# A two-block network on one core: two attentions get lanes of their own, memory rows another queue, and gathers are counted by their indices

## The chip, the core and the metric

The program runs on one core of a Trainium2 chip. Its engines are TensorE (PE; its weight loads are PEld), VectorE (DVE), ScalarE (ACT), GpSimd (POOL) and SyncE (SP), each with a queue of its own that is worked off in order; transfers are started from SP's, ACT's or POOL's queue and run on 16 DMA engines. The metric is the time of one execution in microseconds of device time.

## What is computed

The input is 256 tokens of width 1024. A first network runs two layers (retention, then differential attention), each followed by a product-key expert layer; a second network then runs gated linear attention (GLA) and latent attention (MLA) side by side, cross attention to a memory of 256 rows, and a feed-forward block. The expert layer picks 8 x 16 = 128 rows of two tables per token:

```python
idx = jnp.take_along_axis(cidx, pos, axis=-1).reshape(PEER_CHUNK, PEER_HEADS * PEER_TOPK)
gate = jax.nn.softmax(top, axis=-1).reshape(PEER_CHUNK, PEER_HEADS * PEER_TOPK)
u_e = jnp.take(u, idx, axis=0)
v_e = jnp.take(v, idx, axis=0)
act = jax.nn.gelu(jnp.einsum('ted,td->te', u_e, xc).astype(jnp.float32))
return jnp.einsum('te,ted->td', (gate * act).astype(v_e.dtype), v_e)
...
o_mla = from_heads(causal_block_attention(q, k, v))
h = h + jnp.concatenate([o_gla, o_mla], axis=-1) @ w_out[l]
hn = rms_norm(h, norm_xa[l])
mn = rms_norm(mem, norm_mem[l])
```

## The kernel before, in words

Tokens are worked in two tiles of 128. The expert layers make four phases of 128 slots each: layer 0 of tile 0 and of tile 1, then layer 1 of tile 0 and of tile 1. A slot gathers one row of u and v side by side for each of 128 tokens (tile `g`, 128 x 2048 floats, 1.05 MB) by an indirect DMA from POOL (line 1103). There are eight `g` buffers; in the last phase one of them holds `xr`, so seven serve gathers. A slot then passes three stations. DVE multiplies the u half with the token and sums it (`g,pd<-g,xr`, line 1122; called a dot below). For each pair of slots ACT makes the gelu's terms (`pd<-pd`, lines 1125 and 1128), DVE the weight (`pw`, line 1137), and ACT two diagonal matrices from it (`dg`, line 1143). PE adds the v halves to the output with them (`Y<-g,dg`, line 275), and after that the buffer is free and POOL may issue the next gather.

Everything else runs beside these phases: routing, both attentions of layer 1, and in the last phase the memory's keys and values (`mem_kv`), the entry to the second network for tile 0 (`c_open`), and tile 0's GLA and MLA. Each of these is a Python generator in a lane. While the program is built, `experts` chooses after each step what comes next from a model of the engines (`Clock`): a ready dot, a ready `pw` with its products (`sums`), or a step of a side lane whose own data are ready by the model. What it chooses is the fixed order of each engine's queue. After a step the lane's wait time is set by what the generator yielded: a weight's job, a constant (LC), or nothing, which means the end of everything the step wrote.

In `mem_kv` one step both starts the load of 128 memory rows (`mx`, from SP, line 1332) and puts their squaring (`rms,ss<-mx`, line 625) into ACT's queue; a later step puts the reciprocal root on DVE (`rsqrt`, lines 352 to 366) and the scaling by it on ACT (line 628). `c_gla` and `c_mla` of tile 0 are one lane, zipped: each step of the lane takes a step of both, and inside `c_gla` the gates' products are zipped with `gla`. `rot` in `mla` (a product and six rope instructions on DVE, lines 1767 and 1386 to 1391) is part of a single step.

After the last phase tile 1 goes through `c_open`, GLA, MLA and, zipped with them, the rest of tile 0; cross attention and feed-forward follow. PE also gets filler products into an accumulating bank (`Y<-cst,zero`, line 271) where the model sees it idle.

Of the kernel before, what the change touches and what calls it, by code (L numbers as in the profile page):

```python
# [18 lines left out]
T = 256  # L19
# [151 lines left out]
LC, HP = 1, 2  # L171
# [5 lines left out]
QUEUE = 2.0  # L177
# [104 lines left out]
class Net:  # L282
# [560 lines left out]
    def route_open(self, t, l):  # L843
        if t == l == 0:
            xT = yield from self.xT_of(self.X[t], gain=self.col("ln_g0"), off=self.col("ln_b0"))
        elif t == l:
            xT = yield from self.xT_of(self.X[t])
        elif l == 0:
            xT = self.tl("om", D, name="rxT").rearrange("p (b t) -> p b t", b=8)
            yield from self.transp(self.X[t], xT, 8)  # L850
        else:
            xT = self.tl("om", D, name="rxT").rearrange("p (b t) -> p b t", b=8)
            yield from self.transp(self.X[t], xT, 8)
        idx = self.tl("idx", 128, I32, bufs=2)
        gate = self.tl("gate", 128, bufs=2)
        self.routed[t, l] = [idx, gate, 0, xT]
        yield

    def pq0_first(self):
# [72 lines left out]
    def route_t(self, t, l, s2, heads=(0, 1)):  # L932


        nc, V = self.nc, self.nc.vector
        idx, gate, n0, _ = self.routed[t, l]
        nh = len(heads)
        nb, ns = 2 * nh, 16 * nh
        sc = s2[:, :nb * 128].rearrange("p (b n) -> p b n", b=nb)
# [45 lines left out]
        to = lambda a, s, j: a[64 * s:64 * s + 64, n0:n0 + ns].rearrange("p (q j) -> p q j", j=2)[:, :, j]  # L985
        for s, j, _, r, c in spots:
            V.scalar_tensor_tensor(to(idx, s, j), part[0][r, c], float(NK), part[1][r, c], op0=OP.mult, op1=OP.add)
        ga = self.small(ns, name="ga").rearrange("p (h k) -> p h k", h=nh)
        V.tensor_tensor(ga, top, top[:, :, 0:1].to_broadcast([128, nh, 16]), op=OP.subtract)
        nc.scalar.activation(ga, ga, AF.Exp)  # L990
# [5 lines left out]
        gf = ga.rearrange("p h k -> p (h k)")  # L996
        for s, j, _, r, c in spots:
            V.tensor_scalar(to(gate, s, j), gf[r, c], gs[r, s * nh // 2:s * nh // 2 + 1], None, op0=OP.mult)
        self.routed[t, l][2] = n0 + ns
        yield  # L1000

    def route(self, t, l, i, heads=(0, 1)):
# [43 lines left out]
    def experts(self, phases, first, beside):  # L1046
# [4 lines left out]
        nc, V, clk = self.nc, self.nc.vector, self.clk  # L1051
        seq = [(p, n) for p in range(len(phases)) for n in range(NSLOT)]
        rows, ph, got = {}, {}, []
        done = 0
# [23 lines left out]
        def step(lane):  # L1078
            s = lanes[lane][0]
            clk.end = 0.0  # L1080
            c = next(s["gen"], self)
            if c is self:
                over.add(s["name"])
                lanes[lane].pop(0)
                return
            s["job"] = c if isinstance(c, tuple) else None
            s["wait"] = clk.free["PE"] - QUEUE if c == LC else clk.end

        def routed(p):
            t, l = phases[p][:2]  # L1090
# [71 lines left out]
        while c < len(seq) or pairs or tail:  # L1162
            while fetched < len(seq) and fetch(fetched):
                fetched += 1
            now = clk.free["DVE"]
            ways = []
            if tail:
                ways.append((max(now, max(clk.ready(a) for a in ph[tail[0]]["y"])), 0, close))
            if pairs and "th" in pairs[0] and not (tail and seq[pairs[0]["c"]][1] == 0):
                ways.append((max(now, clk.ready(pairs[0]["th"])), 1, sums))  # L1170
            if c < fetched and not (seq[c][1] == 0 and c - done > 4):
                ways.append((max(now, clk.ready(rows[c])), 2, lambda: dot(c)))
            at, kind, do = min(ways, key=lambda x: x[:2], default=(math.inf, 0, None))
            side = open_lanes()
            if do:
                lag = now - clk.ready(rows[c]) if c < fetched else 0.0
                short = fetched < len(seq) and seq[fetched][1] >= routed(seq[fetched][0])
                side = [s for s in side if s[0] <= at and lag < (LATE if short or s[1] - c < NEAR else LAG)
                        and clk.free["PE"] - at < QUEUE]
                if side:  # L1180
                    step(min(side, key=lambda s: s[1:])[1 + 1])
                    continue
                do()
                c += kind == 2
            else:
                assert side, (c, fetched, {k: [s["name"] for s in v] for k, v in lanes.items()})
                step(min(side)[2])
# [136 lines left out]
    def mem_kv(self):  # L1324
# [4 lines left out]
        mT = []  # L1329
        for m in range(2):  # L1330
            x = self.s4("mx")
            nc.sync.dma_start(x, self.a["mem"][m * 128:(m + 1) * 128, :])
            o = yield from self.rms(x)
            mT.append(self.s4("mT").rearrange("p (k t) -> p k t", k=8))
            yield from self.transp(o, mT[m], 8, gain=self.col("norm_mem_2"))
# [171 lines left out]
    def c_gla(self, t):  # L1507
# [13 lines left out]
            yield from self.lin_w("win", 2, [(p, False, xT, 0, 512)])  # L1521
            yield from self.silu2(p, sog, half=rs[2])

        yield from self.zip(self.gla(t, aT, gqk, gv, sog, om, rs), gates())

    def c_mid(self, t, rs, hT):

# [207 lines left out]
    def mla(self, t, cqkv, cT, om, cr):  # L1735
# [29 lines left out]
        def rot(a, g):  # L1765
            x = a[:, :, 64:96]
            V.tensor_tensor(x, x, self.vec(g)[:, None, 64:].to_broadcast([128, 8, 32]), op=OP.mult)
            self.rope2(x, t)

        def prep_q():  # L1770
            r = self.head_rs(qf, 8, 96, 96 ** -0.5)
            next(r)
            next(r)
            yield
            rot(q, "mla_q_norm_2")
            yield
            yield from self.transp(qf, qT.rearrange("p (b t) -> p b t", b=8), 8, cols=96, scale=self.col("mla_q_norm_2")[:96])
            qs.append((yield from r))
# [1 line left out]
        def prep_k():  # L1780
# [2 lines left out]
            next(r)  # L1783
            next(r)
            yield
            rot(kk, "mla_k_norm_2")
            rk = yield from r
            V.tensor_tensor(kk, kk, rk[:, :, None].to_broadcast([128, 8, 96]), op=OP.mult)
            yield
# [104 lines left out]
    def all(self):  # L1894
# [12 lines left out]
        def blocks(l, jobs):  # L1907
# [3 lines left out]
            for t, i, heads, by in jobs:  # L1911
# [17 lines left out]
            (1, 0): [S(270, "ln11", self.ln_b(1, 1)), S(348, "b1", self.stage_b(1)), S(354, "open11", self.route_open(1, 1)),  # L1929
                     *blocks(1, [(1, i, both, 368 + 32 * i) for i in range(4)])],  # L1930
            (0, 1): [S(440, "mem", self.mem_kv()), S(480, "c_open", self.c_open(0), names("P", 1, 1)),
                     S(520, "attn", self.zip(self.c_gla(0), self.c_mla(0)), names("T", 1, 1))]})
        self.gctx.close()
        self.fp = self.ctx2.enter_context(self.tc.tile_pool(name="f", bufs=1))
        f8 = lambda n: self.fp.tile([128, 2 * D], F32, tag="hi", name=n, bufs=5)
# [72 lines left out]
```

## Time and profile before

| | us |
|---|---|
| median of 3 runs (lowest to highest) | 2110.01 (2107.73 to 2110.71) |
| the profiled execution | 2110.49 |
| its span, first to last instruction | 2108.6 |
| PE busy | 1793.1 (85%) |
| DVE busy | 1466.8 (70%) |
| ACT busy | 710.1 (34%) |
| POOL busy | 593.6 (28%) |

The mean granted TensorE clock is 0.962 of full speed. Transfers move 708.54 MB, 540.25 MB of them on POOL's queue, at a mean of 336 GB/s over the span. PE's busy time holds fillers (347.1 us) and modelled ends, so it is no sign that PE is the bound; the stages have different limits and are read one by one.

### The profile page before, as it was taken

What the parts mean: (1) busy time and instruction counts of PE and PEld (TensorE: products, weight loads), DVE (VectorE), ACT (ScalarE), POOL (GpSimd) and SP (SyncE); (2) the same over time, 40 slices, a digit from 0 to 9 for tenths busy, and PEclk for the clock granted to TensorE, in tenths of its full rate; (3) what the DMA queues carried; (4) which work ended last, traced back from release to release, by engine and by line L of the source; (5) the groups of instructions that cost most, each with busy time, mean ns of one, the idle gap of its engine ahead of it and who ended that gap; (6) DMA issues with size and microseconds to landing.
All of it is one profiled execution on the core that took longest, in us unless ns stands there. A gap on an engine that the chain in (4) does not pass through costs nothing. (4 is left out here: it accounts for less than half of the span.)

```text
span 2108.6 us, 29190 instructions
## 1 busy us (share of the span) xinstructions
PE 1793.1 (85%) x10022; PEld 1184.0 (56%) x10022; DVE 1466.8 (70%) x3984; ACT 710.1 (34%) x1852; POOL 593.6 (28%) x523
## 2 busy tenths in 40 slices
PE   8999688777788899777989888678988777888999
PEld 8877555454443546554345466444434443668998
DVE  7766898888853666898447678956656655566776
ACT  4443233323332332223234322322334323443443
POOL 0000344444442343334334423323424440000000
PEclk9999899999999999999999999989999998899999
DMA  8654899999999999999999999979999996034554
GB/s 291 233 170 145 336 405 418 409 419 407 418 418 417 392 414 415 415 417 391 417 417 412 418 414 413 371 270 413 417 373 361 408 416 210 31 100 140 190 180 140
DMA packets 123907, 708.54 MB, mean 336 GB/s; under 512 B 14305, under 2 KB 17393, under 8 KB 57969
## 3 DMA queue, kind: packets, MB, share of 16 engines
q0 software_dynamic: 74480, 540.25, 62.8%
q1 hardware_dynamic: 46512, 157.77, 21.0%
q10 hardware_dynamic: 2768, 8.68, 1.1%
q8 instruction: 80, 1.31, 0.2%
q14 instruction: 67, 0.54, 0.1%
HBM read 705.59 MB, written 1.05 MB: 335 GB/s over the span
## 5 line engine op out<-in xcount | busy, mean ns | idle before, releaser
L1103 POOL DMA_INDIRECT g<-d_uv,idx x512 | 589.6, 1152 | 1138.0 <-PE Y L275 555.7
L1122 DVE SCALAR_TENSOR_TENSOR g<-g,xr 128x1024 f32<-128x1024 f32 x512 | 625.3, 1223 | 344.9 <-DMA g<-d_uv,idx 324.1
L275 PE MATMUL Y<-g,dg 128*64 128x512 f32 x2048 | 535.3, 643 | 253.9 <-ACT dg L1143 252.6
L275 PEld LDWEIGHTS Y<-g,dg 128*64 128x64 f32 x2048 | 140.7, 142 | 484.0 <-ACT dg L1143 365.0
L271 PEld LDWEIGHTS Y<-cst,zero 128*64 128x64 f32 x2784 | 316.5, 139 | 103.4 <-issue 98.7
L271 PE MATMUL Y<-cst,zero 128*64 128x128 f32 x2784 | 347.1, 277 | 0.0
L1143 ACT ACTIVATE dg<-cst,pw 128x64 f32<-128x64 f32 x512 | 152.4, 340 | 345.0 <-DVE pw L1137 302.6
L1125 ACT ACTIVATE pd<-pd 128x2 f32<-128x2 f32 x256 | 52.0, 203 | 558.2 <-DVE g L1122 558.1
L392 ACT ACTIVATE hi<-w 128x1024 fp32r<-128x1024 f32 x144 | 147.2, 1055 | 133.0 <-DMA w<-d_up 33.1
L659 DVE TENSOR_TENSOR wl<-w,hi 128x1024 fp32r<-128x1024 f32 x107 | 129.9, 1223 | 65.4 <-ACT hi L392 48.8
L1128 ACT ACTIVATE pd<-pd 128x1 f32<-128x1 f32 x512 | 170.5, 380 | 8.6
L275 PE MATMUL m<-w,xT 128*128 128x512 f32 (+1 forms) x320 | 152.0, 611 | 0.0
L275 PE MATMUL m<-f,hi 128*128 128x256 f32 x704 | 125.3, 282 | 0.0
L275 PEld LDWEIGHTS m<-f,hi 128*128 128x128 f32 x704 | 109.6, 191 | 0.7
L275 PEld LDWEIGHTS m<-w,xT 128*128 128x128 f32 x320 | 58.5, 195 | 73.8 <-issue 68.1
L275 PE MATMUL m<-f,wl 128*128 128x256 f32 x264 | 74.2, 281 | 0.0
L659 DVE TENSOR_TENSOR lo<-w,hi 128x1024 fp32r<-128x1024 f32 x37 | 45.3, 1223 | 23.6 <-ACT hi L392 23.5
L1137 DVE SCALAR_TENSOR_TENSOR pw<-pd 128x2 f32<-128x2 f32 x256 | 38.5, 151 | 26.1 <-ACT pd L1128 24.3
L275 PEld LDWEIGHTS m<-xT,w 128*128 128x128 f32 (+1 forms) x416 | 47.7, 190 | 12.6 <-issue 9.6
L275 PE MATMUL m<-xT,w 128*128 128x128 f32 (+1 forms) x416 | 52.0, 283 | 0.2 <-ACT xT L392 0.2
L275 PE MATMUL m<-hi,xh 128*128 128x512 f32 x128 | 51.4, 401 | 0.0
L275 PE MATMUL m<-hi,xl 128*128 128x512 f32 x128 | 50.1, 391 | 0.0
(445 smaller groups left out, 2377.9 us busy)
## 6 DMA issues: line engine op xcount, KB each, us to landing
w<-d_retin SPq DMA_DIRECT2D x48, 512.0 KB, 5.0
w<-d_pq SPq DMA_DIRECT2D x40, 512.0 KB, 15.8
w<-d_kvw SPq DMA_DIRECT2D x32, 512.0 KB, 12.2
w<-d_gate SPq DMA_DIRECT2D x22, 512.0 KB, 4.3
w<-d_up SPq DMA_DIRECT2D x22, 512.0 KB, 3.9
w<-d_down SPq DMA_DIRECT2D x22, 512.0 KB, 4.3
w<-d_win SPq DMA_DIRECT2D x21, 512.0 KB, 7.7
w<-d_retout SPq DMA_DIRECT2D x16, 512.0 KB, 4.0
```

The lines of the kernel that those rows point to most:

```text
L271: net.nc.tensor.matmul(net.open_y[:64, :128], net.zero.to_broadcast([128, 64]), net.ident, start=False, stop=False)
L275: self.net.nc.tensor.matmul(out, a, b, start=start, stop=stop)
L392: self.nc.scalar.activation(o, i, AF.Copy, scale=scale)
L659: self.nc.vector.tensor_tensor(lo[:, c], x[:, c], hi[:, c], op=OP.subtract)
L1103: nc.gpsimd.indirect_dma_start(out=g, out_offset=None, in_=self.a[f"uv{l}"], in_offset=bass.IndirectOffsetOnAxis(ap=self.routed[t, l][0][: ...
L1122: V.scalar_tensor_tensor(g[:, :D], g[:, :D], GELU_C, ph[p]["xr"][:, n % 2], op0=OP.mult, op1=OP.mult, accum_out=d[:, n % 2:n % 2 + 1])
L1125: nc.scalar.activation(s, d, AF.Square, scale=math.sqrt(0.044715) / GELU_C)
L1128: nc.scalar.activation(th[:, j:j + 1], s[:, j:j + 1], AF.Tanh, scale=e, bias=e)
L1137: V.scalar_tensor_tensor(w, q["th"], 1.0, q["gd"], op0=OP.add, op1=OP.mult)
L1143: nc.scalar.activation(dg, self.c("eye2"), AF.Copy, scale=w[:, j:j + 1])
```

## The change

Five things are edited. (1) Tile 0's GLA and MLA become two lanes, G and M: M starts after `c_open`, G after `c_open` and the last routing. In G the gates' products come before `gla`, not zipped with it (tile 1 keeps the zip). (2) `rot` yields after the product and after the rope, for both tiles. (3) The memory rows are loaded from ACT's queue, and the step ends there: the generator yields the tile `x`, and the lane then waits for the model's landing of just that tile. (4) The count of slots whose index is ready is raised right after the indices are written, before the gates; a second count, raised after the gates, now guards the dots. (5) `step` understands a yielded tile.

```diff
@@ route_t
             V.scalar_tensor_tensor(to(idx, s, j), part[0][r, c], float(NK), part[1][r, c], op0=OP.mult, op1=OP.add)
+        self.routed[t, l][2] = n0 + ns
...
-        self.routed[t, l][2] = n0 + ns
+        self.routed[t, l][4] = n0 + ns
@@ experts
-            s["wait"] = clk.free["PE"] - QUEUE if c == LC else clk.end
+            s["wait"] = clk.ready(c) if isinstance(c, bass.AP) else clk.free["PE"] - QUEUE if c == LC else clk.end
...
-            if c < fetched and not (seq[c][1] == 0 and c - done > 4):
+            if c < fetched and not (seq[c][1] == 0 and c - done > 4) and seq[c][1] < self.routed[phases[seq[c][0]][:2]][4]:
@@ mem_kv
-            nc.sync.dma_start(x, self.a["mem"][m * 128:(m + 1) * 128, :])
+            nc.scalar.dma_start(x, self.a["mem"][m * 128:(m + 1) * 128, :])
+            yield x
             o = yield from self.rms(x)
@@ c_gla
-        yield from self.zip(self.gla(t, aT, gqk, gv, sog, om, rs), gates())
+        if t:
+            yield from self.zip(self.gla(t, aT, gqk, gv, sog, om, rs), gates())
+        else:
+            yield from gates()
+            yield from self.gla(t, aT, gqk, gv, sog, om, rs)
@@ mla
             V.tensor_tensor(x, x, self.vec(g)[:, None, 64:].to_broadcast([128, 8, 32]), op=OP.mult)
+            yield
             self.rope2(x, t)
+            yield
@@ all
-                     S(520, "attn", self.zip(self.c_gla(0), self.c_mla(0)), names("T", 1, 1))]})
+                     ("G", 505, names("T", 1, 1) | {"c_open"}, "gla", self.c_gla(0)),
+                     ("M", 510, {"c_open"}, "mla", self.c_mla(0))]})
```

The order of POOL's queue does not move at all, and SP's only by the two memory loads. DVE, ACT and PE keep their order up to slot 6 of the last phase; from there it differs. The line numbers of the changed kernel are 1 to 8 higher.

First place: DVE in the last phase around slot 18, at the second block of memory rows. `rx` to `ry` with 128x1 are the reciprocal root. Before:

```order
L1122 SCALAR_TENSOR_TENSOR g,pd<-g,xr 128x1024 x2
L1129 TENSOR_TENSOR pd<-pd,gate 128x2
L1122 SCALAR_TENSOR_TENSOR g,pd<-g,xr 128x1024
L352 TENSOR_SCALAR rx<-ss 128x1
L354 TENSOR_SCALAR rh<-rx 128x1
...
L366 SCALAR_TENSOR_TENSOR ry<-rt,ry 128x1
L1137 SCALAR_TENSOR_TENSOR pw<-pd 128x2 x3
L387 TENSOR_TENSOR mT<-m,cols 128x512
L1122 SCALAR_TENSOR_TENSOR g,pd<-g,xr 128x1024
```

The same place in the changed kernel:

```order
L1123 SCALAR_TENSOR_TENSOR g,pd<-g,xr 128x1024
L1138 SCALAR_TENSOR_TENSOR pw<-pd 128x2
L352 TENSOR_SCALAR rx<-ss 128x1
L354 TENSOR_SCALAR rh<-rx 128x1
...
L366 SCALAR_TENSOR_TENSOR ry<-rt,ry 128x1
L1123 SCALAR_TENSOR_TENSOR g,pd<-g,xr 128x1024
L1130 TENSOR_TENSOR pd<-pd,gate 128x2
L1123 SCALAR_TENSOR_TENSOR g,pd<-g,xr 128x1024
L387 TENSOR_TENSOR mT<-m,cols 128x512
L1138 SCALAR_TENSOR_TENSOR pw<-pd 128x2
```

Three `pw` stood behind seven dots and the root; now each `pw` stands behind the next pair's first dot. Counted over DVE's whole queue, the dots ahead of a `pw` less the slots already summed are 2 or 3 at 253 of the 256 `pw` before, 5 at two and 7 at one, all three at the memory rows; in the changed kernel they are 2 or 3 at all 256.

Second place: DVE in the attention of tile 0, around slot 65 before and slot 71 now (`la` is GLA's gate, `mq` and `mk` with `dr` are `rot`). Before:

```order
L1634 SCALAR_TENSOR_TENSOR la<-m,rs_11191,vecs 128x256
L1640 TENSOR_SCALAR la<-la 128x256
...
L1122 SCALAR_TENSOR_TENSOR g,pd<-g,xr 128x1024
L1129 TENSOR_TENSOR pd<-pd,gate 128x2
L1651 TENSOR_TENSOR ke<-m,cum 128x256
L1767 TENSOR_TENSOR mq<-mq,vecs 128x8x32
...
L1391 TENSOR_TENSOR mk<-dr 128x8x16
L1357 TENSOR_REDUCE hs<-sq 128x4
L1137 SCALAR_TENSOR_TENSOR pw<-pd 128x2
```

In the changed kernel:

```order
L1123 SCALAR_TENSOR_TENSOR g,pd<-g,xr 128x1024
L1640 SCALAR_TENSOR_TENSOR la<-m,rs_11207,vecs 128x256
L1773 TENSOR_TENSOR mq<-mq,vecs 128x8x32
L1773 TENSOR_TENSOR mk<-mk,vecs 128x8x32
L1138 SCALAR_TENSOR_TENSOR pw<-pd 128x2
L1123 SCALAR_TENSOR_TENSOR g,pd<-g,xr 128x1024
L1130 TENSOR_TENSOR pd<-pd,gate 128x2
L1646 TENSOR_SCALAR la<-la 128x256
L1647 TENSOR_TENSOR la<-la,lu 128x256
L1648 TENSOR_SCALAR la<-la 128x256
L1138 SCALAR_TENSOR_TENSOR pw<-pd 128x2
```

All of `rot` (14 instructions) stood between a pair's `pd` and its `pw`; now only short pieces do, and the 12 rope instructions stand behind a dot with a `pw` just ahead of them.

Third place: PE between the `Y` products of slots 61 and 63, in the changed kernel; before, the longest such run was six `m<-w,xT` and four `m<-w,cT`.

```order
L275 MATMUL Y_10194<-g,dg 64x512 x2
L275 MATMUL m<-w,cT 128x512 x2
L275 MATMUL m<-w,xT 128x512 x8
L271 MATMUL Y_10193<-cst,zero 64x128 x2
L275 MATMUL m<-w,cT 128x256 x2
L275 MATMUL Y_10193<-g,dg 64x512 x2
```

The run grew by two `m<-w,xT`. Over the program PE has 49 fillers fewer, 1343 for 1392.

## Rows read from the trace of the kernel before

**Rows 1.** The page, part 2: GB/s in 40 slices.

```profile
GB/s 291 233 170 145 336 405 418 409 419 407 418 418 417 392 414 415 415 417 391 417 417 412 418 414 413 371 270 413 417 373 361 408 416 210 31 100 140 190 180 140
```

**Rows 2.** Windows by stage: engines busy (instructions), granted clock, DMA share, GB/s.

```profile
core 0: us, PE busy (x) PEld busy (x) DVE busy (x) ACT busy (x) POOL busy (x), PEclk, DMA share, GB/s
1370.00:1430.00 60.00, 46.99 (x265) 29.50 (x263) 32.27 (x91) 16.13 (x47) 18.29 (x18) 0.88 0.76 280
1430.00:1575.00 145.00, 127.60 (x555) 60.54 (x554) 85.19 (x236) 49.85 (x150) 53.53 (x46) 0.99 1.01 418
1575.00:1640.00 65.00, 52.32 (x286) 29.82 (x284) 46.75 (x131) 24.56 (x83) 26.75 (x24) 0.92 0.85 328
1640.00:1735.00 95.00, 68.72 (x426) 41.82 (x424) 56.23 (x138) 29.23 (x99) 43.43 (x41) 0.98 1.01 418
```

**Rows 3.** Timeline, POOL: start us, us, instruction [idle before <-releaser].

```profile
1418.15 0.94 POOL L1103 DMA_INDIRECT g<-d_uv,idx  x1 [14.35 <-PE Y L275]
...
1552.65 1.96 POOL L1103 DMA_INDIRECT g<-d_uv,idx  x1 [6.66 <-PE Y L275]
...
1580.51 0.95 POOL L1103 DMA_INDIRECT g<-d_uv,idx  x1 [15.06 <-PE Y L275]
...
1720.43 0.94 POOL L1103 DMA_INDIRECT g<-d_uv,idx  x1 [2.38 <-PE Y L275]
```

**Rows 4.** Timeline of DVE and ACT at the second block of memory rows.

```profile
1411.34 1.23 DVE L1122 SCALAR_TENSOR_TENSOR g<-g,xr 128x1024 f32<-128x1024 f32 x1 [1.18 <-DMA g<-d_uv,idx]
...
1412.49 0.15 DVE L352 TENSOR_SCALAR rx<-ss 128x1 f32<-128x1 f32 x1
...
1414.33 0.23 DVE L1137 SCALAR_TENSOR_TENSOR pw<-pd 128x2 f32<-128x2 f32 x2
...
1414.45 1.15 ACT L628 ACTIVATE rms<-mx,ry 128x1024 f32<-128x1024 f32 x1 [3.55 <-DVE ry L366]
...
1415.51 0.57 ACT L1143 ACTIVATE dg<-cst,pw 128x64 f32<-128x64 f32 x2
```

**Rows 5.** Timeline of ACT and DVE in the attention of tile 0.

```profile
1565.91 1.28 ACT L1638 ACT_TABLE_LOAD   x1
...
1574.16 0.41 DVE L1767 TENSOR_TENSOR mq<-mq,vecs 128x256 f32<-128x256 f32 x1
...
1578.22 0.15 DVE L1137 SCALAR_TENSOR_TENSOR pw<-pd 128x2 f32<-128x2 f32 x1
```

**Rows 6.** Windows: the change from phase 2 to phase 3.

```profile
960.00:1000.00 40.00, 30.22 (x158) 17.29 (x158) 35.06 (x89) 15.88 (x46) 19.58 (x16) 0.87 0.96 384
```

**Rows 7.** Tile mx (min/median/max): the memory rows' issues, and all its landings.

```profile
L1332 SPq DMA_DIRECT2D mx<-d_mem x2: 328/350/372, 1315.5 to 1387.4; - x2
DMA to landing us min/median/max: 3.3/9.5/15.6
```

**Rows 8.** Windows: the 25 us around POOL's longest wait.

```profile
1565.00:1590.00 25.00, 21.13 (x105) 12.53 (x104) 17.49 (x55) 13.30 (x34) 5.56 (x6) 0.93 0.75 293
```

**Rows 9.** Timeline of PE: weight products between two pairs of Y.

```profile
1546.90 1.88 PE L275 MATMUL m<-w,xT 128*128 128x512 f32 x4
```

**Rows 10.** Timeline of PE in the attention of tile 1.

```profile
1791.81 1.08 PE L279 MATMUL m<-cst,gqk 128*128 128x128 f32 x4 [4.49 <-DVE gqk L1659]
```

**Rows 11.** Timeline of PE: equal products after two different idle times.

```profile
1358.49 1.94 PE L275 MATMUL Y<-g,dg 128*64 128x512 f32 x8 [2.96 <-ACT dg L1143]
...
1366.46 3.68 PE L275 MATMUL Y<-g,dg 128*64 128x512 f32 x8 [6.04 <-ACT dg L1143]
```

**Rows 12.** Groups by form, 1340 to 1760 us: PE's busy us, mean ns.

```profile
L275 PE MATMUL Y<-g,dg 128*64 128x512 f32 x544 | 146.0, 657 | 80.2 <-ACT dg L1143 80.2
L275 PE MATMUL m<-w,mT 128*128 128x512 f32 x64 | 29.0, 600 | 0.0
L275 PE MATMUL m<-w,xT 128*128 128x512 f32 x48 | 23.3, 608 | 0.0
L275 PE MATMUL m<-w,xT 128*128 128x416 f32 x32 | 14.6, 582 | 0.0
```

More of the change, by code (lines that the diff above doesn't have):

```diff
@@ L855, in route_open @@
         gate = self.tl("gate", 128, bufs=2)
-        self.routed[t, l] = [idx, gate, 0, xT]
+        self.routed[t, l] = [idx, gate, 0, xT, 0]
         yield
@@ L935, in route_t @@
         nc, V = self.nc, self.nc.vector
-        idx, gate, n0, _ = self.routed[t, l]
+        idx, gate, n0 = self.routed[t, l][:3]
         nh = len(heads)
@@ L1774, in prep_q @@
             yield
-            rot(q, "mla_q_norm_2")
+            yield from rot(q, "mla_q_norm_2")
             yield
@@ L1785, in prep_k @@
             yield
-            rot(kk, "mla_k_norm_2")
+            yield from rot(kk, "mla_k_norm_2")
             rk = yield from r
```

## The prediction, made before the changed kernel ran

> **What bounds the kernel now.** I read the page's second part first, in 40 slices of 52.7 us. There the transfers run at 391 to 419 GB/s in nearly all slices from the sixth to the thirty-third, and what falls out of that is short: 371 and 270 where the last phase starts, then 373 and 361 [rows 1]. The gathers are thus the bound wherever their loop runs unbroken. At 1.05 MB a slot and 418 GB/s a pair of slots costs 5.0 us, and no engine needs that long for its share of a pair. So a stage's loss is its length times what its rate lacks of 418.
>
> Windows by stage then place the loss [rows 2]. From 1430 to 1575 and from 1640 to 1735 us the rate is the full 418 GB/s. From 1370 to 1430, with the memory rows, it is 280: 60 x (1 - 280/418) = 19.8 us lost. From 1575 to 1640, in tile 0's attention, it is 328: 65 x (1 - 328/418) = 14.0 us lost. Together 33.8 us, and the gathers' end pulls everything behind it, since tile 1's second network needs the last slot.
>
> POOL's timeline shows how it is lost. Each pair costs POOL a wait of some 2.4 us for a free buffer when all is well; 6.66 us still passed inside the full-rate stage; but there are waits of 14.35 and 15.06 us [rows 3]. Both name a `Y` as releaser, so PE came late, and the question is what held PE.
>
> In the memory rows it is DVE's order [rows 4]. A dot ends at 1412.6, then comes the reciprocal root for the memory rows, and only at 1414.33 the three `pw` of pairs whose dots had long been done. ACT waits 3.55 us for the root, scales the rows, and starts `dg` at 1415.51. The root waits for nothing, so the memory rows had landed and been squared by then: the rows were not late, the order was. In the attention two things stand between a pair's `pd` and its `pw` [rows 5]: a table load of 1.28 us on ACT, and all of `rot`, from 1574.16 to 1578.22, 4.1 us of DVE.
>
> **The change, part by part.** The sum stands against the profiled execution, 2110.49 us, 0.5 us over the median.
>
> *Memory rows.* After the yield the lane waits by the model for the load alone and no step holds load and squaring together. In the order now printed each `pw` stands one dot behind its own pair, in both blocks. That removes the cause of the 14.35 us wait, and I take back the 19.8 us but for two terms. First, refilling after a phase change costs something whatever the order: at the change from phase 2 to 3, with no memory rows, the rate was 384 over 40 us, 40 x (1 - 384/418) = 3.3 us [rows 6]; I keep 3.3. Second, the squaring now stands in ACT's queue near its load, with ACT's `pd` and `dg` of the next pairs queued behind it, and `pw`, `Y`, POOL wait for those. Rows under full load took 15.6 us to land at most and 3.3 at least [rows 7]. ACT's order has about two pairs of work, 10.0 us, between the second load and its squaring; at 15.6 us ACT stands 5.6 us. On top of POOL's usual 2.4 that is a wait of 8.0 us.
>
> What does a wait cost? Around the 15.06 us wait the rate over 25 us was 293, so 25 x (1 - 293/418) = 7.5 us were lost, and the first 15.06 - 7.5 = 7.6 us were covered by gathers already in flight [rows 8]. A wait of 8.0 us so costs 0.4 us. The bounds are 0 (landing in 3.3 us) and the same 0.4. In the first block the gap is two and a half pairs, 12.5 us: 3.1 us late, covered. Memory part: 19.8 - 3.3 - 0.4 = 16.1 us.
>
> *The load's issue.* It costs 0.33 to 0.37 us of SP's time each [rows 7]. On ACT I take the same, 0.7 us for both, on an engine that works 16.13 of 60 us there [rows 2]: nothing, and SP, whose next loads come sooner by as much, gains nothing. Were ACT's cover gone, it would cost 0.7.
>
> *Lanes and `rot`.* In the new order no `pw` of the whole program stands behind more than the next pair's first dot, so the 4.1 us of `rot` leave the chain. What is late next is PE: its longest run between two pairs' `Y` grew by two `m<-w,xT`, which the trace counts as four, each product being two passes there: 1.88 us [rows 9]. The longest wait that passed free was 6.66; 6.66 + 1.88 = 8.5, less 7.6 is 0.9 us lost. A table load stays in one pair's chain: 1.3 us [rows 5]. Both bounds: nothing, if they fall in a covered wait, and 2.2 together. Attention part: 14.0 - 0.9 - 1.3 = 11.8 us.
>
> *Indices before gates.* POOL's order is unchanged, and the gather read only the indices before too; I price the count at nothing. If gates had bound it, a gather could come sooner by at most the pieces of one step, and the loop's buffers, not the indices, end POOL's waits [rows 3].
>
> *The tail.* Behind the last gather the instructions are the same; some of tile 1's change places. The nearest row is a transpose that waits 4.49 us for `gqk`, which now comes sooner [rows 10]; what one reorder can give another can take, so the bounds are -4.5 and +4.5, and I take 0.
>
> Sum: 16.1 + 11.8 = 27.9 us, so 2110.49 - 27.9 = 2082.6 us, call it 2083.
>
> **The rivals.** *A: only the memory rows get better.* In the new order the attention's side work ends about slot 105, where it ended about slot 96; if the planner's model errs there as it erred before, a stall forms elsewhere and costs the same 14.0. Then 2110.49 - 16.1 = 2094.4. For it: the model has erred at 15.06 us once. Against: no late `pw` is left in the order.
>
> *B: the memory stretch loses the same.* If the landing of `mx`, not the order, is what everything there waits for, the wait moves to ACT and the 19.8 us stay: 2110.49 - 11.8 = 2098.7. For it: landings up to 15.6 us. Against: the root found its input ready [rows 4]. What separates B from the forecast is whether the yield, which changes the order, or the landing decides. The Trainium skill, "DMA: Bandwidth & Descriptors", section "Issuing engines are not separate DMA queues", says that transfers started by ScalarE, SyncE or GpSimd run on the same 16 engines and interleave, so another engine's queue saves only the sequencer's time to start them. By that rule the rows land no sooner from ACT and the moved queue alone gives at most its issue, 0.7 us: were the queue the whole repair, the time would be B's. No row of before shows a load from ACT's queue under the gathers, so it is not borne out or refuted here.
>
> *C: slower, by PE's clock.* The same eight products took 1.94 us after 2.96 us of idle time and 3.68 after 6.04 [rows 11]: the second is the 1.2 GHz level, the first 2.4. The change takes out 49 fillers, so PE may idle oftener. PE's four largest groups without fillers take 146.0 + 29.0 + 23.3 + 14.6 = 212.9 us from 1340 to 1760 [rows 12]; at the lower level throughout, twice that, 425.8. The gathers run from 1340 to about 1735 [rows 2], 395 us, less 27.9 is 367. PE would then be the bound by 59 us: 2141. It decides from where 212.9 x (1 + f) passes 367, at f = 0.72 of the products on the lower level, and makes the kernel slower than before where it passes 395, at f = 0.86. The Trainium skill, "TensorE: Matmul & The Clock Gate", section "Part 1: The HAM clock gate", says that the throttled state is the default and activity releases it; the pair of products agrees, 3.68 for 1.94 us, and by that rule fillers taken out could cost more than they took. Against C: where the loop ran unbroken the granted clock was 0.99 and 0.98, and it was the stalls that had 0.88 and 0.92 [rows 2]; fewer stalls should raise it.
>
> *D: nothing moves.* Both stalls form again next door, 2110.
>
> **How the numbers follow.** Forecast 0.70, A 0.13, B 0.06, C 0.04, D 0.03; better than the range 0.04. All 33.8 recovered gives 2076.7, and with the tail's 4.5 some 2072; upward A and B stand at 2094.4 and 2098.7. I take 2075 to 2099, which leaves out C, D and the lowest corner. A measurement of this kernel tells about 0.2%, 4 us, from no change. Faster is forecast, A, B and the corner, 0.93; same is D, 0.03; slower is C, 0.04.
>
> **What would show it.** Right: in the windows of the two stretches about 400 GB/s where 280 and 328 stood; no POOL wait over 9 us in the last phase but at its start; the last gather's issue some 28 us earlier, and the time from there to the end unchanged within 4.5 us; `pw` one dot behind its pair at the memory rows; a granted clock near 0.98 in both stretches. A shows as a wait over 10 us between slots 60 and 105, B as ACT's squaring waiting on `mx` for over 7 us, C as `Y` products of 3.7 us in rows. Wrong altogether would be a tail longer by more than 5 us, since nothing in my sum would account for it.

## The result, and the profile of the changed kernel

The changed kernel takes 2087.14 us in the median of four runs (2086.5 to 2088.9), against 2109.64 for the kernel before; the ratio is 0.9896, with a 95% interval of 0.9879 to 0.9913, so 18 to 26 us are gone. The forecast was 2083. The profiled execution took 2087.37 us and its span fell from 2108.6 to 2085.6. These 23.0 us can be followed stage by stage.

The page's slices first. It is the line that answers to [rows 1]:

```profile
GB/s 293 232 173 151 312 401 418 410 419 410 418 410 416 412 403 416 415 417 390 418 417 408 420 414 416 404 363 417 414 417 379 412 407 177 36 118 148 184 186 117
```

Where 371, 270, then 373 and 361 stood, there are now 404, 363, then 379 and 412. Windows over the stretches of [rows 2], same columns (the gathers end earlier now, so the last one is cut at 1715):

```profile
1370.00:1430.00 60.00, 48.90 (x249) 26.79 (x245) 40.92 (x113) 20.58 (x62) 27.59 (x23) 0.93 0.98 404
1430.00:1575.00 145.00, 130.04 (x553) 60.94 (x553) 87.13 (x241) 50.08 (x152) 53.29 (x48) 0.97 1.01 414
1575.00:1640.00 65.00, 55.85 (x317) 32.85 (x316) 48.74 (x137) 27.89 (x94) 28.81 (x26) 0.93 0.96 390
1640.00:1715.00 75.00, 55.27 (x342) 33.13 (x338) 45.42 (x113) 22.81 (x77) 33.76 (x33) 0.98 1.01 414
```

The memory rows' stretch went from 280 to 404 GB/s, worth 60 x (404 - 280)/418 = 17.8 us, and the attention's from 328 to 390, worth 65 x (390 - 328)/418 = 9.6 us. The stretch between them lost 145 x (418 - 414)/418 = 1.4 us that it had not lost before. On the timeline of PE the last `Y` of a slot starts 25.5 us earlier, before and now:

```profile
1738.92 1.94 PE L275 MATMUL Y<-g,dg 128*64 128x512 f32 x8 [0.84 <-ACT dg L1143]
```

```profile
1713.47 1.94 PE L275 MATMUL Y<-g,dg 128*64 128x512 f32 x8 [0.84 <-ACT dg L1144]
```

This is the gain of the gathers in this one profile; in the second profile of the same kernel, below, it is 18.4 us.

POOL's timeline of the changed kernel has one wait of over 7.5 us left between 1370 and 1720 us, where [rows 3] had 14.35 and 15.06:

```profile
1429.46 0.94 POOL L1104 DMA_INDIRECT g<-d_uv,idx  x1 [6.75 <-PE Y L275]
...
1549.05 0.94 POOL L1104 DMA_INDIRECT g<-d_uv,idx  x1 [10.12 <-PE Y L275]
...
1567.44 0.94 POOL L1104 DMA_INDIRECT g<-d_uv,idx  x1 [5.15 <-DVE hs L1359]
...
1576.14 0.94 POOL L1104 DMA_INDIRECT g<-d_uv,idx  x1 [6.11 <-PE Y L275]
```

At the second block of memory rows, the timeline of ACT and DVE shows what became of [rows 4]. `rms<-mx` is the squaring, whose rows were asked for at 1395.57:

```profile
1406.38 1.04 ACT L625 ACTIVATE rms<-mx 128x1024 f32<-128x1024 f32 x1
...
1407.94 0.16 DVE L1138 SCALAR_TENSOR_TENSOR pw<-pd 128x2 f32<-128x2 f32 x1
...
1408.01 0.15 DVE L352 TENSOR_SCALAR rx<-ss 128x1 f32<-128x1 f32 x1
...
1409.86 1.22 DVE L1123 SCALAR_TENSOR_TENSOR g<-g,xr 128x1024 f32<-128x1024 f32 x1
```

`pw` stands ahead of the root, one dot behind its pair. The squaring has no idle time ahead of it: the rows had landed within 10.8 us, and ACT stood for nothing.

Behind the gathers nothing was forecast to change, within 4.5 us. From the last `Y` to the last `xoT`, the end of cross attention's first stage, it was 1895.79 - 1738.92 = 156.9 us and is 1865.57 - 1713.47 = 152.1, a gain of 4.8. The last `xoT` before and now:

```profile
1895.79 0.69 DVE L659 TENSOR_TENSOR xoT<-m,xoT 128x512 fp32r<-128x512 f32 x1 [1.05 <-ACT xoT L392]
```

```profile
1865.57 0.69 DVE L659 TENSOR_TENSOR xoT<-m,xoT 128x512 fp32r<-128x512 f32 x1 [1.05 <-ACT xoT L392]
```

From the first `hh` of the feed-forward to the end, the window was 173.6 us and is 181.1, a loss of 7.5. So 25.5 + 4.8 - 7.5, and 0.3 between, make up the span's 23.0 us. Neither of the last two terms stood in the sum of the forecast, and the experiments ask after them too.

### The profile page after: what moved, and what is told of

It reads as the page before. It is cut to its first block, busy times and chain, and to the rows that moved or that the text cites. A ratio compares the mean times of both kernels' runs of the same rounds, so it can differ in the third digit from the quotient of the medians.

```text
span 2085.6 us, 28994 instructions
## 1 busy us (share of the span) xinstructions
PE 1789.3 (86%) x9924; PEld 1181.5 (57%) x9924; DVE 1466.3 (70%) x3984; ACT 709.0 (34%) x1852; POOL 592.6 (28%) x523
## 5 line engine op out<-in xcount | busy, mean ns | idle before, releaser
L271 PEld LDWEIGHTS Y<-cst,zero 128*64 128x64 f32 x2686 | 311.4, 141 | 106.2 <-issue 101.4
L275 PE MATMUL m<-w,xT 128*128 128x512 f32 (+1 forms) x320 | 147.4, 600 | 0.0
```

The source lines that it names most:

```text
L271: net.nc.tensor.matmul(net.open_y[:64, :128], net.zero.to_broadcast([128, 64]), net.ident, start=False, stop=False)
L275: self.net.nc.tensor.matmul(out, a, b, start=start, stop=stop)
```

## The experiments

All ratios are to runs of the kernel before on the same chip beside them; brackets hold 95% intervals. The count (indices, not gates) was not run by itself: in the printed order the kernel before with this edit alone has the same instructions in the same places on all five engines as without it, and the changed kernel without it the same as with it. So it does nothing to this program. Two of the runs below (the memory edits and rot without the lanes, and the zip) are without it.

### The memory rows: the yield alone

```diff
             nc.sync.dma_start(x, self.a["mem"][m * 128:(m + 1) * 128, :])
+            yield x
-            s["wait"] = clk.free["PE"] - QUEUE if c == LC else clk.end
+            s["wait"] = clk.ready(c) if isinstance(c, bass.AP) else clk.free["PE"] - QUEUE if c == LC else clk.end
```

> Only the yield behind the memory rows' load (and the wait on that one tile); the load stays on SP's queue, the attention as before. DVE's order then has no pw behind more than one dot of the next pair. Order theory (what the changed kernel's trace suggests: 404 GB/s for 280 between 1370 and 1430 us, so 60 x (404 - 280)/418 = 17.8 us): gathers end 17 to 18 us sooner, the time falls by 15 to 19 us to about 2092, and POOL has no wait over 9 us before slot 50. Rival, the landing or the queue decides: the wait moves to ACT's squaring, the time stays within 4 us of 2110.

Measured: 2095.94 us against 2109.69, ratio 0.9927 [0.9910, 0.9943]. The windows of the memory rows and of the attention:

```profile
1370.00:1430.00 60.00, 48.24 (x250) 26.29 (x247) 40.81 (x113) 20.91 (x63) 28.08 (x23) 0.95 0.98 398
1575.00:1640.00 65.00, 52.66 (x280) 28.83 (x280) 45.30 (x124) 26.44 (x89) 28.38 (x24) 0.92 0.89 352
```

The memory stretch is repaired with the loads still on SP's queue, and the attention's long wait (14.71 us on POOL's timeline) stands. The time fell by 14 us, a little under the 15 to 19 expected, with an interval of 12 to 19 us. In the profile, which is of the slowest of its six executions (2101.03 us), the last `Y` starts at 1727.89, only 11.0 us sooner than before and not 17 to 18: the memory rows gained 60 x (398 - 280)/418 = 16.9 us, but from 1430 to 1575 the rate was 400 GB/s for 418, which costs 6.2.

### The memory rows: the queue alone

```diff
-            nc.sync.dma_start(x, self.a["mem"][m * 128:(m + 1) * 128, :])
+            nc.scalar.dma_start(x, self.a["mem"][m * 128:(m + 1) * 128, :])
```

> Only the queue: the two memory loads start from ACT, nothing else moves. Order theory: the 14.35 us wait of POOL stands as before, the rate from 1370 to 1430 stays near 280 GB/s and the time within 2 us of 2110. Rival, the queue is the repair: rate about 400 there and the time near 2092.

Measured: 2109.06 us, ratio 1.0006 [0.9995, 1.0017]. The window and POOL's wait are those of before:

```profile
1370.00:1430.00 60.00, 47.61 (x262) 29.14 (x259) 32.94 (x92) 16.00 (x47) 19.90 (x18) 0.85 0.72 282
...
1419.18 0.94 POOL L1103 DMA_INDIRECT g<-d_uv,idx  x1 [14.51 <-PE Y L275]
```

The queue's gain is nothing that can be measured, at most 0.05% by the interval. It did change something on ACT, where the squaring now stood right behind its own load and waited for the rows:

```profile
1378.53 1.06 ACT L625 ACTIVATE rms<-mx 128x1024 f32<-128x1024 f32 x1 [5.97 <-DMA mx<-d_mem]
...
1408.01 1.06 ACT L625 ACTIVATE rms<-mx 128x1024 f32<-128x1024 f32 x1 [7.09 <-DMA mx<-d_mem]
```

The second is the sign that I had named for rival B, a squaring that waits over 7 us for `mx`, and it cost nothing that the time shows. The Trainium skill, "DMA: Bandwidth & Descriptors", section "Issuing engines are not separate DMA queues", has it that another engine's queue saves only the time of starting a transfer; the unchanged time agrees with that. That the transfers share their DMA engines, which the page states too, is not shown by this run.

### The attention's edits, the memory rows as before

The edit is all of the change's (1) and (2), here in short:

```diff
-                     S(520, "attn", self.zip(self.c_gla(0), self.c_mla(0)), names("T", 1, 1))]})
+                     ("G", 505, names("T", 1, 1) | {"c_open"}, "gla", self.c_gla(0)),
+                     ("M", 510, {"c_open"}, "mla", self.c_mla(0))]})
...
+            yield from gates()
+            yield from self.gla(t, aT, gqk, gv, sog, om, rs)
...
+            yield
             self.rope2(x, t)
+            yield
```

> Only the attention's edits (two lanes, gates ahead of gla for tile 0, rot's yields); memory rows as before. Order theory: memory stretch 280 GB/s as before; the attention's stretch gains what the changed kernel gained there, 65 x (390 - 328)/418 = 9.6 us less some 1.8 us of smaller losses elsewhere, so gathers end 7 to 10 us sooner; the tail is then 1 to 3 us longer than before, as in the changed kernel: 2101 to 2105 us. Rival, the two gains are not separate (the attention's stretch is only better because the side work starts from another slot): time within 4 us of 2110. A sum of this and of the yield alone that meets the changed kernel's 22.5 us says they add.

Measured: 2098.86 us against 2109.69, ratio 0.9944 [0.9925, 0.9964], some 11 us less and lower than the 2101 to 2105 expected.

```profile
1370.00:1430.00 60.00, 45.98 (x261) 28.41 (x258) 32.10 (x91) 16.36 (x47) 21.28 (x18) 0.83 0.72 264
1575.00:1640.00 65.00, 53.41 (x310) 31.25 (x310) 51.41 (x143) 28.28 (x83) 29.02 (x24) 0.95 0.98 395
```

Within the intervals the two gains add: the yield's 0.73% and the attention's 0.56% make 1.29%, and the whole change has 1.04% and, run again, 1.15%. But the gain does not lie where I had it. In the profile the last `Y` starts at 1734.01, 4.9 us sooner than before and not 7 to 10, while from there to the last `xoT` it takes 149.5 us for 156.9. So more than half of this run's gain is of the tail, which I had expected to lengthen by 1 to 3 us.

### rot's yields in tile 1 alone

```diff
-            self.rope2(x, t)
+            if t: yield
+            self.rope2(x, t)
+            if t: yield
```

(`rot` is then called with `yield from`, as in the change.)

> rot yields in tile 1 alone, so only the program behind the last gather moves. In the changed kernel tile 1's attention ends 5.0 us sooner against the last gather than before (its cross attention stands 30.5 us earlier, the gathers ended 25.4 earlier), and the feed-forward then takes 7.1 us longer. Theory L (the feed-forward's length depends on how its weight loads happen to land, not on the order): the attention gains 5 us here too, and the feed-forward takes anything from 167 to 175 us: time 2105 to 2112. Rival T (the reorder gains nothing, the weights set the end): cross attention 5 us sooner, feed-forward 5 us longer, time within 1 us of 2110. Rival N: no gain in the attention without the earlier gathers' end.

Measured: 2103.68 us, ratio 0.9972 [0.9959, 0.9985], so 3 to 9 us less and a little below the 2105 to 2112 expected, with the gathers ending where they ended before. PE's transposes of `gqk`, which waited 4.49 us in [rows 10], in this kernel and in the changed one:

```profile
1788.36 0.77 PE L279 MATMUL m<-cst,gqk 128*128 128x128 f32 x4 [1.71 <-DVE gqk L1659]
```

```profile
1762.64 0.77 PE L279 MATMUL m<-cst,gqk 128*128 128x128 f32 x4 [1.70 <-DVE gqk L1665]
```

With `rot` cut into steps, DVE makes `gqk` ahead of a root and a reduction that stood before it; 2.8 us of the wait go, and what is behind follows. From the last `Y` to the last `xoT` it is 1891.36 - 1739.05 = 152.3 us here, as in the changed kernel. The feed-forward took 173.5 us, so nothing gave this gain back. Rival T, the weights set the end, falls.

The 13 profiles of this study agree. From the last `Y` to the last `xoT` it takes 149.5 to 152.8 us in the eight whose tile 1 has the yields, and 156.3 to 158.4 in the five whose tile 1 has not, whatever else they hold.

### The change without tile 1's yields

```diff
+            if not t: yield
             self.rope2(x, t)
+            if not t: yield
```

> The changed kernel with rot's yields in tile 0 alone, so tile 1's attention stands as in the kernel before. Theory (the tail's gain comes from tile 1's rot yields alone; the profiled feed-forward of the changed kernel, 181.0 us from its first hh to the end against 173.5 in four other profiles, was one execution's weight landings): cross attention again some 155 us behind the last Y, feed-forward 173 to 176 us in the profile, time 4 to 7 us over the changed kernel's, 2091 to 2094. Rival (the feed-forward is long in the changed kernel because it starts after a shorter attention): feed-forward 173.5 and time within 1 us of the changed kernel's 2087.

Measured: 2087.94 us against 2107.53, ratio 0.9905 [0.9890, 0.9920]. The stages came as the theory has it: 1868.20 - 1711.92 = 156.3 us to the last `xoT`, and a feed-forward of 174.0. But the time is not 4 to 7 us over the changed kernel's: it is within 1 us of it, which with that feed-forward is what the rival had named. Executions of one kernel differ by 5 us and more in these runs, and the two intervals overlap, so this pair of times settles nothing. That a shorter attention makes the feed-forward long falls by other profiles: six more kernels have the shorter attention, and their feed-forward takes 173.3 to 175.4 us. That tile 1's yields shorten the way to the last `xoT` rests on the 13 profiles and the run before.

### rot alone, and the lanes alone

Against the kernel before, the first has only

```diff
+            yield
             self.rope2(x, t)
+            yield
```

(again with `yield from` at the calls of `rot`) and the second only

```diff
+                     ("G", 505, names("T", 1, 1) | {"c_open"}, "gla", self.c_gla(0)),
+                     ("M", 510, {"c_open"}, "mla", self.c_mla(0))]})
...
+            yield from gates()
+            yield from self.gla(t, aT, gqk, gv, sog, om, rs)
```

> rot's yields for both tiles and nothing else. DVE's longest work between a pd and its pw in the attention falls as in the changed kernel, one lane as before. Theory (rot between pd and pw was the attention stretch's loss): the 15.06 us wait falls by about rot's 4.1 us, gathers end 3 to 5 us sooner than before, tile 1 gives the 6 us that its yields gave alone: 2099 to 2102. Rival (the lanes give it): only tile 1's 6 us, 2103 to 2105.

> Two lanes and the gates ahead of gla, rot in one step, memory rows as before. rot then stands in another pair's chain. Theory: a wait over 12 us remains in the attention, the gathers end within 3 us of before, time 2106 to 2111. Rival (the lanes give the attention's gain): rate near 390 in the attention's stretch and 2101 to 2105.

Measured: rot's yields alone 2100.75 us, ratio 0.9968 [0.9957, 0.9980]; the lanes alone (with the gates ahead of `gla`) 2106.18, ratio 0.9991 [0.9981, 1.0001]. Each against 2107.53. The attention's window of the one and of the other:

```profile
1575.00:1640.00 65.00, 55.04 (x297) 30.65 (x296) 50.47 (x147) 27.89 (x91) 26.17 (x24) 0.95 0.91 356
```

```profile
1575.00:1640.00 65.00, 54.64 (x316) 32.38 (x315) 49.83 (x141) 30.55 (x97) 26.46 (x24) 0.95 0.95 378
```

In the times rot has what tile 1 alone gave (0.9968 and 0.9972), and the lanes have nothing clear of noise. In the windows each repairs a part: 356 and 378 GB/s for 328, and 395 together. With rot alone the long wait fell to 11.33 us and the last `Y` starts 4.2 us sooner, as the theory had it; the time, 4 to 9 us less, does not part theory and rival. With the lanes alone the last `Y` starts 5.8 us sooner, where I had said within 3. My expectation that a wait over 12 us remains in the attention was wrong too: POOL's longest there is 9.87 us. The trace of before suggests why, in rows that I had not read. DVE and ACT in the same pair as [rows 5]:

```profile
1571.56 1.28 ACT L1128 ACT_TABLE_LOAD   x1
...
1573.43 0.36 ACT L392 ACTIVATE cum<-m 128x256 f32<-128x256 f32 x1
...
1573.82 0.42 DVE L1651 TENSOR_TENSOR ke<-m,cum 128x256 f32<-128x256 f32 x1 [2.32 <-ACT cum L392]
1574.16 0.41 DVE L1767 TENSOR_TENSOR mq<-mq,vecs 128x256 f32<-128x256 f32 x1
```

The zipped lane put a GLA step, `ke`, and an MLA step, `rot`, into one pair's chain, and `ke` stood 2.32 us for a `cum` that waited behind a table load. The lanes part the two, the yields cut the second; both shorten the same chain. This is read from the order and the windows; no run isolates that chain.

What tile 0's attention is worth in time can be estimated from two pairs of runs. The attention's edits with and without tile 0 (0.9944 and 0.9972) and the change without tile 1's yields beside the memory yield alone (0.9905 and 0.9927) differ by 0.28% and 0.22%, so 5 to 6 us. Each of these differences is uncertain by some 0.2%.

### The memory edits and rot, without the lanes

Against the changed kernel:

```diff
-                     ("G", 505, names("T", 1, 1) | {"c_open"}, "gla", self.c_gla(0)),
-                     ("M", 510, {"c_open"}, "mla", self.c_mla(0))]})
+                     S(520, "attn", self.zip(self.c_gla(0), self.c_mla(0)), names("T", 1, 1))]})
```

(and the zip in `c_gla` and the count as before.)

> The changed kernel without its two lanes (and without the count, which moves no instruction): memory yield, ACT's queue, rot's yields. PE's longest run between two pairs of Y falls back from eight to six products of w,xT. Theory (rot carries the attention's gain, the longer PE run costs 10.12 - 7.6 = 2.5 us): 2083 to 2087, not slower than the changed kernel. Rival (the lanes carry it): 2089 to 2093.

Measured: 2092.24 us against 2107.53, ratio 0.9921 [0.9909, 0.9934]. This is the rival's number. The whole change has 0.9896 [0.9879, 0.9913] in its first measurement and 0.9885 [0.9865, 0.9905] in the second, below. The first interval overlaps this run's, the second just doesn't: the lanes probably carry 0.2 to 0.4%. That they cost more than they give, as the theory had it, is not borne out. And the shorter run of weight products did not shorten the long wait, which is 11.33 us here and 10.12 in the changed kernel. The stretches behind the memory rows show the loss:

```profile
1430.00:1575.00 145.00, 127.48 (x549) 59.31 (x550) 87.19 (x248) 50.87 (x152) 52.06 (x47) 0.99 0.99 404
1575.00:1640.00 65.00, 54.84 (x314) 32.11 (x312) 50.53 (x145) 26.86 (x88) 25.57 (x24) 0.95 0.98 388
...
1570.19 1.30 POOL L1103 DMA_INDIRECT g<-d_uv,idx  x1 [11.33 <-PE Y L275]
```

That is 4.9 + 4.7 = 9.6 us lost from 1430 to 1640, for 1.4 + 4.4 = 5.8 in the changed kernel.

### The changed kernel again, with SP's queue, and with the zip

The first has no edit. The others, against the changed kernel, are this one:

```diff
-            nc.scalar.dma_start(x, self.a["mem"][m * 128:(m + 1) * 128, :])
+            nc.sync.dma_start(x, self.a["mem"][m * 128:(m + 1) * 128, :])
```

and this one:

```diff
-            yield from gates()
-            yield from self.gla(t, aT, gqk, gv, sog, om, rs)
+            yield from self.zip(self.gla(t, aT, gqk, gv, sog, om, rs), gates())
```

(with the count as before, too.)

> The changed kernel once more, unedited. Theory J (the feed-forward's length changes from execution to execution with the landing of its weights): this profile shows its feed-forward near 174 us in place of 181.0, with cross attention again 150 us behind the last Y, and the times spread over 5 us or more. Theory S (with this start the feed-forward is always longer): 179 to 182 us again, and all times within 3 us of 2087.

> The changed kernel with its memory rows loaded from SP's queue again; DVE's, PE's and POOL's order are the same. Theory (the queue is worth at most 0.7 us): memory stretch 400 to 411 GB/s as with ACT's queue, time within 2 us of the changed kernel's run beside it. Rival (behind the yield, the queue decides when the squaring's data land): a POOL wait over 9 us between 1370 and 1430 us and a time 3 us or more above. By the feed-forward: theory J gives any length from 173 to 181, theory S 179 to 182.

> The changed kernel with the gates' products zipped with gla again for tile 0 (and without the count, which moves no instruction). PE's longest run of side products before pair 31 stays eight products of w,xT long. Theory (of the attention's edits the gates' order is worth nothing measurable): time within 3 us of the changed kernel's run beside it, attention stretch 380 to 395 GB/s. Rival (it holds what the run without lanes lacked): 3 to 5 us above.

Measured, each against 2109.12 us: the changed kernel again 2085.74 (2082.66 to 2091.47), ratio 0.9885 [0.9865, 0.9905]; with SP's queue 2083.30, 0.9877 [0.9856, 0.9899]; with the gates zipped again 2082.85, 0.9882 [0.9860, 0.9903]. The three can't be told apart, so no effect of the queue or of the gates' order is shown, and no version is shown to beat the changed kernel. POOL's longest wait in the memory stretch of the SP version is under 7.5 us, as with ACT's queue, and the rate there is 397 GB/s, 3 below the range that I had named and the same as in the changed kernel's run beside it.

The changed kernel's second profile, of its slowest execution (2091.47 us), has the gathers end later than the first:

```profile
1640.00:1715.00 75.00, 54.14 (x349) 33.49 (x349) 44.29 (x111) 23.54 (x80) 36.84 (x33) 1.00 0.97 396
...
1720.55 1.94 PE L275 MATMUL Y<-g,dg 128*64 128x512 f32 x8 [0.78 <-ACT dg L1144]
```

That is 7.1 us behind the first profile's 1713.47, with the same order of instructions; the four stretches have 397, 411, 383 and 396 GB/s for 404, 414, 390 and 414. So a single profile places the gathers' end no better than that, and what makes the difference stays open. The stretch behind it agrees with the first profile: 151.6 us to the last `xoT`.

On the feed-forward, these are ACT's `hi<-w` (the split of a weight's rows, columns as on the page) from the first `hh` to the end, in the kernel before, the changed one, and the changed one again:

```profile
L392 ACT ACTIVATE hi<-w 128x1024 fp32r<-128x1024 f32 x58 | 58.4, 1051 | 35.4 <-DMA w<-d_up 29.1 <-PE m L275 3.4 <-PE Y L275 2.2
```

```profile
L392 ACT ACTIVATE hi<-w 128x1024 fp32r<-128x1024 f32 x58 | 58.0, 1050 | 42.0 <-DMA w<-d_up 42.0
```

```profile
L392 ACT ACTIVATE hi<-w 128x1024 fp32r<-128x1024 f32 x58 | 58.1, 1050 | 39.3 <-DMA w<-d_up 39.1 <-DMA w<-d_gate 0.2
```

The same 58 splits, but 29.1, 42.0 and 39.1 us of waiting for `w<-d_up`, with windows of 173.6, 181.1 and 178.7 us. In the other ten profiles of this study the window lies between 173.3 and 175.4. ACT, DVE and PE work through the feed-forward in the same order in all 13. In the changed kernel's first profile the last `hh` came so late that PE stood 3.63 us, and behind that its last products ran partly at the 1.2 GHz level (0.80 us for one that takes 0.39 at the upper one; granted clock 0.90 over the last 35.6 us):

```profile
2073.14 0.80 PE L275 MATMUL O<-hi,hh 128*128 128x512 f32 x1 [3.63 <-ACT hh L392]
```

```profile
2050.00:2085.60 35.60, 27.29 (x153) 23.29 (x151) 18.87 (x30) 8.34 (x11) 0.00 (x0) 0.90 0.26 92
```

So in these three the length of this stage goes with the landing of its `up` weights, which no run moved on purpose, and it differs between executions of the one kernel by 2.4 us at least. Theory J had it near 174 in the second execution, which it was not; theory S had all times within 3 us of 2087 and the SP version at 179 or more, and they spread from 2082.66 to 2091.47, and the SP version has 175.4. Neither is borne out whole. Why the changed kernel's own two profiles both show late weights stays open.

## Why the prediction was right, and where it was off

**What bounds the kernel.** Right in the main. The loss was in two stretches of the gathers' loop, and with both repaired the gathers ended 25.5 us sooner in the first profile, of the 27.9 that I had summed. It was 18.4 us in the second, and with the yield alone 11.0 for the 16.9 that its stretch gained. So the end of the gathers does not follow the repaired stretch alone.

**Memory rows.** Right in mechanism, and the yield alone shows it. I took back 16.1 us and the stretch gave 17.8. Of the two terms held back, the refill of 3.3 was too large: all that the stretch still loses is 60 x (1 - 404/418) = 2.0 us, and 1.0 to 3.0 over the seven profiles with the yield. The squaring's 5.6 us of standing, from a landing of 15.6 us, did not come at all. That landing was of the first load, started at 1315.5 and squared only at 1371; the second, under the gathers of the last phase, had landed in 3.3. From ACT's queue the rows landed 5.5 to 8.3 us after their start in the four profiles of runs with both the yield and that queue that show it.

**The load's queue and the indices.** Priced at nothing, and they are nothing. Rival B, for which the landing or the queue decides, needed the queue to be the repair or the yield to fail; two runs show neither. Its sign, a wait of the squaring, came with the queue alone and without a price.

**Lanes and rot.** The step that was mis-sized. I had 11.8 us and the stretch gave 9.6: it still loses 65 x (1 - 390/418) = 4.4 us where I kept 2.2. The pairs of runs above give 5 to 6 us, uncertain by some 4. The failing step is the price of PE's longer run, 1.88 us added to the 6.66 that had passed free. That run is sixteen products in the trace, and behind it on ACT two evictions stand ahead of `dg`:

```profile
1539.07 7.03 PE L275 MATMUL m<-w,xT 128*128 128x512 f32 x16
...
1543.38 0.16 DVE L1138 SCALAR_TENSOR_TENSOR pw<-pd 128x2 f32<-128x2 f32 x1
...
1546.13 0.69 ACT L392 ACTIVATE V<-m,rs 128x512 f32<-128x512 f32 x1 [5.49 <-PE m L275]
...
1546.72 0.68 ACT L392 ACTIVATE mq<-m,ry 128x512 f32<-128x512 f32 x1
...
1547.29 0.58 ACT L1144 ACTIVATE dg<-cst,pw 128x64 f32<-128x64 f32 x2
```

I had added the four products to PE and forgotten who queues on ACT for them: the `dg` of a pair whose `pw` was done at 1543.5. POOL's wait is 10.12 us, not 8.5. Nor was the price of a wait a sum over single waits: the windows just behind this one run at full rate, and the dip comes at 1565, when the waits of 5.15 and 6.11 follow.

```profile
1540.00:1565.00 25.00, 24.36 (x82) 10.20 (x81) 9.52 (x21) 7.87 (x24) 6.35 (x6) 1.00 1.02 419
1565.00:1575.00 10.00, 6.97 (x44) 4.43 (x45) 7.70 (x20) 7.70 (x19) 2.28 (x2) 0.92 1.00 392
1575.00:1590.00 15.00, 14.68 (x87) 8.43 (x84) 10.93 (x32) 5.29 (x18) 9.45 (x8) 0.94 0.85 332
```

I read this so: what gathers in flight can cover is spent by the first long wait, and short ones behind it then cost. No run tests it by itself. Two table loads, at 1571.88 and 1574.18, stand there; I had one.

The trace of before already spoke against the price and against the cause that I had found. The 15.06 us wait with its 7.5 us was only half of the 14.0 that the stretch lost. A second wait, which [rows 3] leave out, stands behind it, with a `pw` that came after a root and other attention work on DVE, and that stretch lost 50 x (1 - 363/418) = 6.6 us where my price for 9.81 us of waiting is 2.2:

```profile
1590.00:1640.00 50.00, 40.25 (x230) 23.31 (x229) 34.03 (x88) 18.59 (x64) 21.65 (x20) 0.93 0.93 363
...
1617.17 0.15 DVE L1137 SCALAR_TENSOR_TENSOR pw<-pd 128x2 f32<-128x2 f32 x1
...
1620.02 1.80 POOL L1103 DMA_INDIRECT g<-d_uv,idx  x1 [9.81 <-DVE pw L1137]
```

I had taken this half back without having found what caused it. That most of it came back in the changed kernel, which loses 50 x (1 - 407/418) = 1.3 us from 1590 to 1640, is luck as far as my working goes.

**The tail.** The step that failed in kind. I looked for what moved and found the wait for `gqk`, but took 0 with 4.5 to either side. Tile 1's yields gave 4.8 us between the last `Y` and the last `xoT`, and alone 3 to 9 us of time. It was a gain to be counted, since the order put `gqk` ahead of work that nothing waited for. The feed-forward's 7.5 us the other way are not explained by the change: other kernels with the same order there show 173.3 to 175.4 us, the changed kernel's two profiles 181.1 and 178.7. The attention's gain that I had too large, the tail's that I had left out and this loss partly cancel, so that 2083 came so near to 2087 is in part luck.

**The rivals.** A's sign, a wait over 10 us in the attention, did appear by 0.12 us, but not its price: the stretch loses 4.4 us, not 14.0. My sign was wrong: a wait of 10 us does not mean that the stretch is lost. For C, the clock did not rise to 0.98 as I had said: the two stretches have 0.93 each, from 0.88 and 0.92. C's price did not come, but the clock was not free either. Ahead of the end of POOL's 6.11 us wait the eight `Y` of a pair took 3.33 us, behind 3.03 us of idle time, where they take 1.94 at the upper level and 3.68 at the lower [rows 11]:

```profile
1573.88 3.33 PE L275 MATMUL Y<-g,dg 128*64 128x512 f32 x8 [3.03 <-ACT dg L1144]
```

D and the slower side are excluded by the interval.

## What to carry to other kernels

Where a planner fixes the order from a model, look in the trace for an instruction that stands ahead of ready work and itself waits for nothing: it was modelled as late, and a finer step in the source moves it. When such a step is cut, read every place that it is called from, since the same yield gave 5 us in tile 1, where it was not looked for. Before a gain is put down to a queue, run the queue alone.

## What the runs showed that was not expected

A stage whose instructions and order are the same in 13 profiles took from 173.3 to 181.1 us, and in the three shown that goes with how long ACT waited for one of its three weights (29.1 to 42.0 us). In the span of this kernel that is 0.4%, as much as some of the edits. The gathers' end differed by 7.1 us between two profiles of the changed kernel. So one profile's total is no measure of such an edit, one stage of one profile not always either, and what several kernels' profiles share, as the way to the last `xoT` does, is the firmer reading.
